# Gates, branches and output projection of a decoder block formed by tokens, residual and second norm by token halves

## The chip, the cores and the metric

One core of a Trainium2 chip runs the kernel. The metric is device time in microseconds of one execution, as a median of several runs. The engines that matter here are TensorE (PE in the profile, with PEld for its weight loads), VectorE (DVE), ScalarE (ACT) and the queue of SyncE (SPq), which issues most transfers. All of them run their own instruction lists in order and wait for each other by semaphores. Results of TensorE go to PSUM banks of 128 x 512 float32.

## The reference

One decoder block on 256 tokens of width 2048, in float32:

```python
xn = rmsnorm(x, norm_mix_pre)
proj = einsum('bsd,dc->bsc', xn, w_in)
mq, mk, mv, mo, mi, mf, aq, ak, av, g_m, g_a = split_cols(proj)
h_m = (normed mLSTM of conv(mq, mk), mv, mi, mf) * sigmoid(mo)
h_a = block attention of rope(aq), rope(ak), av
merged = sigmoid(g_m) * (h_m @ w_branch_m) + sigmoid(g_a) * (h_a @ w_branch_a)
x = x + rmsnorm(merged @ w_out, norm_mix_post)
u = square(relu(rmsnorm(x, norm_ffn_pre) @ w_up))
x = x + rmsnorm(u @ w_down, norm_ffn_post)
```

The widths: mq, mk, mv, mo, aq, ak, av are 1024 each, the gates g_m and g_a, merged and the output 2048 each, u 8192.

## The kernel before

Every float32 product is made of three products of a higher and a lower part (hi x hi, lo x hi, hi x lo) in a format that TensorE takes fast. So each weight unit of 1 MB (128 x 2048) is loaded by SyncE's queue into one of three raw buffers, ACT casts each half to whi (L169), and DVE subtracts to get wlo (L170). There are four buffers for each, so the weights run one to two units ahead of TensorE.

A product is made in one of two forms. In the feature form (`mm_feat`), the weights are the stationary side and 256 tokens the moving side, hi and lo of the activations side by side: one 512-column matmul (L188) and one of 256 (L189) for each 128 input features. The result has output features on partitions and tokens along the row. `mm_feat_one` does the same with three 256-column matmuls (L215 to L217), into one half of a bank. In the token form (`mm_tok`, L200 to L205), 128 tokens are the stationary side and 512 output columns of the weights the moving side: three 512-column matmuls for each 128 input features and token half. Its result has tokens on partitions; rms scales per token are then per-partition scalars, and whoever wants the features on partitions has to transpose.

The steps run one after another: the products of av, of q and k with attention head by head, of mv, mo, mq, mk with the mLSTM, then gates (`gate_post`), branches (`branch_step`) and the output projection (`feat_step(wo[c], mgmov, ...)`). Before, mo, both gates, both branches and the output projection are in the feature form, one unit of 128 output features at a time. Merged activations come out as needed by the output projection, which has them as its moving side. The sums of squares of its output over features are formed on TensorE with a column of ones. After the last unit (`last_mix`), the scale 1/rms is formed (sums, square root on ACT, a Newton step on DVE), broadcast by a product with the identity (L291), while `keep_warm` puts products of ones (L144) on TensorE. `residual` then goes over 16 feature blocks and makes the normed input hw of the MLP, and the first four up-units run interleaved behind it. `x1_squares` sums the squares for the second norm on TensorE, and `open_mlp` transposes the residual to tokens (L745), 32 transposes. The MLP's down products use seven products instead of eight per group (`group`), a token form with factors xs; the change leaves it as it is, except for the buffers that it takes.

The order on each engine is set by a scheduler, which follows the program's dependences and expected times; what is marked with `keep_in_program_order` keeps its place among the marked instructions. ACT needs another function table for Sin, for Sqrt and for Exp (ACT_TABLE_LOAD); a tiny square root named warm (L678) brings Sqrt's table in ahead of the first use.

## Time and profile before

| | |
|---|---|
| median of 3 runs | 1439.17 us (1438.96 to 1439.21) |
| profiled execution, own time | 1440.65 us |
| its span in the profile | 1438.9 us |
| mean granted TensorE clock | 0.998 of full speed |
| TensorE busy | 1415.9 us (98%) |
| DVE busy | 1148.0 us (80%) |
| ACT busy | 816.2 us (57%) |
| moved by DMA | 281.65 MB, 196 GB/s |

The table says how full each engine is. A full engine is not an engine at its peak, since ends of matmuls are modelled; so the distance from one matmul's start to the next is what a pace is read from. The chain of work that ended last says which engine the end of the span depended on, and the idle time ahead of a group of instructions says what it waited for.

### The profile page before, as it was taken

The page shows a single profiled execution, that of the slowest core. Times are in us where ns is not written, and L with a number is a line of the kernel's source. Part 1 is how long each engine was busy: PE and PEld are TensorE (multiplying, and loading weights), DVE is VectorE, ACT ScalarE, POOL GpSimd, SP SyncE. Part 2 cuts the span into 40 slices and gives each one's busy share as a digit, 9 for nine tenths or more (in the row PEclk, how much of TensorE's full clock was granted, in tenths as well). Part 3 has the DMA queues.
Part 4 walks back from the last instruction along what each step waited for, and adds up shares of the span by engine and source line. Part 5 has one row for each costly group of instructions (what it writes and reads, how often), then busy time and mean ns, then how long its engine had stood idle before and what let it go on. Part 6 is the DMA issues. An engine that isn't in the chain of part 4 may idle for free.

```text
span 1438.9 us, 21795 instructions
## 1 busy us (share of the span) xinstructions
PE 1415.9 (98%) x8578; PEld 1253.8 (87%) x8578; DVE 1148.0 (80%) x1607; ACT 816.2 (57%) x1200; POOL 14.5 (1%) x26
## 2 busy tenths in 40 slices
PE   9999999999999999999999999999999999999997
PEld 7888888888888888888899989989889898888975
DVE  7777766776676666665687899898999989999985
ACT  7655465565555444455656565564655655565561
POOL 0000000000000000000000000000000000000000
PEclk9999999999999999999999999999999999999999
DMA  8644444444445545555627665657646667665651
GB/s 258 218 176 176 174 165 161 175 174 176 176 176 182 200 177 195 184 183 197 236 76 247 236 216 179 253 197 263 226 151 242 219 217 239 212 205 193 237 202 59
DMA packets 44167, 281.65 MB, mean 196 GB/s; under 512 B 5024, under 2 KB 7328, under 8 KB 11424
## 3 DMA queue, kind: packets, MB, share of 16 engines
q1 hardware_dynamic: 41904, 265.57, 49.6%
q0 software_dynamic: 2016, 14.68, 5.5%
q8 instruction: 67, 1.10, 0.3%
q14 instruction: 36, 0.29, 0.1%
q10 hardware_dynamic: 144, 0.01, 0.0%
HBM read 278.14 MB, written 2.10 MB: 195 GB/s over the span
## 4 chain that ended last, share of the span: by engine, by line
PE 85%; DVE 11%; issue 2%; ACT 1%; DMA 1%; SPq 0%; DVEq 0%; ACTq 0%
PE acc L188 27%; PE acc L189 14%; PE acc L217 7%; PE acc L215 7%; PE acc L216 7%; DVE wlo L170 6%; PE acc L232 5%; PE acc L226 5%; PE acc L230 5%; PE acc L200 2%; PE acc L205 2%; PE acc L204 2%; DVE xs L774 1%; DVE rawl L862 1%; ACT whi L169 1%
## 5 line engine op out<-in xcount | busy, mean ns | idle before, releaser
L169 ACT CAST whi<-raw 128x1024 fp32r<-128x1024 f32 (+2 forms) x420 | 425.3, 1017 | 420.1 <-PE acc L188 179.1
L170 DVE TENSOR_TENSOR wlo<-raw,whi 128x1024 fp32r<-128x1024 f32 (+2 forms) x420 | 495.0, 1181 | 208.4 <-ACT whi L169 198.0
L188 PE MATMUL acc<-xw,whi 128*128 128x512 f32 x1152 | 408.9, 395 | 0.0
L189 PE MATMUL acc<-xw,wlo 128*128 128x256 f32 x1152 | 328.6, 285 | 0.0
L217 PE MATMUL acc<-hw,wlo 128*128 128x256 f32 x992 | 279.9, 283 | 4.9 <-DVE wlo L170 4.9
L216 PE MATMUL acc<-hw,whi 128*128 128x256 f32 x992 | 279.2, 282 | 0.0
L215 PE MATMUL acc<-hw,whi 128*128 128x256 f32 x992 | 277.7, 282 | 0.0
L188 PEld LDWEIGHTS acc<-xw,whi 128*128 128x128 f32 x1152 | 216.4, 188 | 50.3 <-issue 2.1
L169 ACT CAST whi<-rawl 128x1024 fp32r<-128x1024 f32 x168 | 173.5, 1048 | 116.8 <-PE acc L216 52.2
L189 PEld LDWEIGHTS acc<-xw,wlo 128*128 128x128 f32 x1152 | 216.7, 188 | 0.9
L170 DVE TENSOR_TENSOR wlo<-rawl,whi 128x1024 fp32r<-128x1024 f32 x168 | 201.8, 1218 | 8.4 <-ACT whi L169 6.5
L217 PEld LDWEIGHTS acc<-hw,wlo 128*128 128x128 f32 x992 | 186.9, 188 | 9.9 <-DVE wlo L170 7.3
L215 PEld LDWEIGHTS acc<-hw,whi 128*128 128x128 f32 x992 | 186.0, 188 | 4.6 <-DVE t L757 0.2
L216 PEld LDWEIGHTS acc<-hw,whi 128*128 128x128 f32 x992 | 186.8, 188 | 2.0
L226 PE MATMUL acc<-whi,xs 128*128 128x512 f32 x440 | 174.8, 397 | 2.9 <-ACT whi L169 2.9
L232 PE MATMUL acc<-wlo,xs 128*128 128x512 f32 x440 | 172.4, 397 | 1.8 <-DVE wlo L170 1.8
L230 PE MATMUL acc<-whi,xs 128*128 128x512 f32 x440 | 173.7, 395 | 0.0
L232 PEld LDWEIGHTS acc<-wlo,xs 128*128 128x128 f32 x440 | 82.6, 188 | 21.0 <-DVE wlo L170 4.5
L226 PEld LDWEIGHTS acc<-whi,xs 128*128 128x128 f32 x440 | 82.7, 188 | 20.7 <-ACT whi L169 6.0
L230 PEld LDWEIGHTS acc<-whi,xs 128*128 128x128 f32 x440 | 82.7, 188 | 18.1
L188 PE MATMUL acc<-mg,whi 128*128 128x512 f32 x240 | 84.2, 393 | 0.0
L189 PE MATMUL acc<-mg,wlo 128*128 128x256 f32 x240 | 67.7, 283 | 0.0
(258 smaller groups left out, 1622.1 us busy)
## 6 DMA issues: line engine op xcount, KB each, us to landing
raw<-in_wi_dram SPq DMA_DIRECT2D x96, 1024.0 KB, 4.8
raw<-in_wu_dram SPq DMA_DIRECT2D x64, 1024.0 KB, 6.2
rawl<-in_wd_dram SPq DMA_DIRECT2D x42, 1024.0 KB, 7.8
raw<-in_wd_dram SPq DMA_DIRECT2D x22, 1024.0 KB, 4.9
raw<-in_wo_dram SPq DMA_DIRECT2D x16, 1024.0 KB, 4.8
rawl<-in_wd_dram POOLq DMA_DIRECT2D x14, 1024.0 KB, 10.7
raw<-in_wa_dram SPq DMA_DIRECT2D x8, 520.0 KB, 4.6
raw<-in_wa_dram SPq DMA_DIRECT2D x16, 256.0 KB, 4.7
```

Of the source, the lines that this page charges most:

```text
L169: S.copy(out=hi[:, s], in_=r)
L170: V.tensor_tensor(out=lo[:, s], in0=r, in1=hi[:, s].bitcast(F32), op=ALU.subtract)
L188: PE.matmul(out=accs[i][:, 0:2 * T], lhsT=hi, rhs=m, start=k == 0, stop=False)
L189: PE.matmul(out=accs[i][:, 0:T], lhsT=lo, rhs=m[:, 0, :], start=False, stop=k == nk - 1)
L200: first = PE.matmul(out=acc, lhsT=m[:, 0, ts], rhs=hi, start=start and k == 0, stop=False)
L204: PE.matmul(out=acc, lhsT=m[:, 1, ts], rhs=hi, start=False, stop=False)
L215: PE.matmul(out=acc, lhsT=hi, rhs=m[:, 0, :], start=k == 0, stop=False)
L216: PE.matmul(out=acc, lhsT=hi, rhs=m[:, 1, :], start=False, stop=False)
L217: PE.matmul(out=acc, lhsT=lo, rhs=m[:, 0, :], start=False, stop=k == KT - 1)
L226: first = PE.matmul(out=acc, lhsT=f[:, k, 0], rhs=hi, start=start and k == 0, stop=False, skip_group_check=more)
L230: PE.matmul(out=acc, lhsT=f[:, k, 1], rhs=hi, start=False, stop=False, skip_group_check=more)
L232: PE.matmul(out=acc, lhsT=f[:, k, 0], rhs=lo, start=False, stop=stop and k == 3, skip_group_check=more)
```

## The change

Mo, both gates, both branches and the output projection go to the token form, with weights laid out for it by the host. The gates' and branches' results use the three small PSUM banks (`sm_tile`) in turn, and the tanh of a gate reads its bank directly, with half the token's 1/rms (rhalf) as scale. Merged activations are transposed in blocks of 512 features (`merged`), after branch m of block 2 for three blocks together and at the end for the fourth. A copy of x by tokens is loaded beside xT (`x1_load`), and the post-norm weights are broadcast to all partitions. Sums of squares come from ACT's accumulator (`square`). The last two weight units of the output projection's last block run half 0 first (24 matmuls), then `residual(0)`, then half 1, then `residual(1)`; each residual adds in four blocks of 512, transposes them, and forms hw's hi on ACT and lo on DVE from PSUM. `first_up` takes two units instead of four. The function `seven_steps` is there but SGATES is empty, so it is never called. Cut to its core:

```diff
+def mo_evac(b, h, acc):
+    S.activation(out=so[b][:, h], in_=acc, func=AF.Tanh, scale=rhalf[:, h:h + 1])
+def gate_steps(c, n):
+    for u in range(4):
+        tok_step(wg["ma".index(n), c, u], ("g", n, c), xmov, u,
+                 lambda h, acc: tanh(gate(n, c)[:, h], acc, h), bank=sm_tile)
+def branch_steps(c, n):
+    def evac(h, acc):
+        g = gt[n, c][:, h]
+        V.scalar_tensor_tensor(out=g, in0=g, scalar=1.0, in1=acc, op0=ALU.add, op1=ALU.mult)
+        if n == "m":
+            V.tensor_tensor(out=g, in0=g, in1=gt["a", c][:, h], op=ALU.add)
+    for u in range(2):
+        tok_step(wbr["am".index(n), c, u], ("b", n, c), lambda k: src[:, k], u, evac, last=1,
+                 bank=sm_tile)
+def merged(c):
+    for q in range(2):
+        ps = sm_tile()
+        for j in range(2):
+            for h in range(2):
+                b = 2 * j + h
+                PE.transpose(out=ps[:, b * P:(b + 1) * P],
+                             in_=src[:, h, (2 * q + j) * P:(2 * q + j + 1) * P],
+                             identity=ident)
+        hi, lo = (m[:, 2 * q:2 * q + 2, i] for i in range(2))
+        p = ps.rearrange("p (k t) -> p k t", t=T)
+        S.activation(out=hi, in_=p, func=AF.Copy, scale=0.5)
+        V.scalar_tensor_tensor(out=lo, in0=p, scalar=0.5, in1=hi.bitcast(F32), op0=ALU.mult,
+                               op1=ALU.subtract)
+both_gates(3, (branch_steps, 1, "m"), (branch_steps, 2, "a"), (branch_steps, 2, "m"))
+then(lambda: [merged(c) for c in range(3)])
+branch_steps(3, "a")
+branch_steps(3, "m")
+then(merged, 3)
...
+def mix_evac(e, h, acc):
+    square(acc, late["ssm"][:, h, e:e + 1])
+    V.tensor_tensor(out=late["mix"][e][:, h], in0=acc,
+                    in1=late["wm"][:, e * 512:(e + 1) * 512], op=ALU.mult)
+    if e == 0 and h == 0:
+        S.activation(out=tiny.tile([P, 2], F32, name="warm", tag="warm"), in_=rhalf,
-            S.activation(out=tiny.tile([P, 2], F32, name="warm", tag="warm"), in_=sq[:, 0:2],
                          func=AF.Sqrt)
+def residual(h):
+    pin = tc.keep_in_program_order
+    mix_evac(3, h, late["acc"][h])
+    rms(v, late["ssm"][:, h])
+    rsqrt_act(r, v, 1)
+    for e in range(5):
+        if e < 4:
+            pin(V.scalar_tensor_tensor(out=x1[:, h, es], in0=late["mix"][e][:, h], scalar=r,
+                                       in1=x1[:, h, es], op0=ALU.mult, op1=ALU.add))
+            ps = late["ps", e] = sm_tile()
+            for j in range(4):
+                PE.transpose(out=ps[:, j * P:(j + 1) * P], in_=x1[:, h, k * P:(k + 1) * P],
+                             identity=ident)
+        for j in range(4) if e else ():
+            S.activation(out=hw[:, k, 0, hs], in_=p, func=AF.Copy, scale=g)
+            pin(V.scalar_tensor_tensor(out=hw[:, k, 1, hs], in0=p, scalar=g,
+                                       in1=hw[:, k, 0, hs].bitcast(F32), op0=ALU.mult,
+                                       op1=ALU.subtract))
+    for e in range(4):
+        square(x1[:, h, e * 512:(e + 1) * 512], late["ss2"][:, h, e:e + 1])
+def last_mix():
+    def mm(units):
+        for h in range(2):
+            for i in range(2):
+                mm_tok(late["acc"], units[i], mgmov, 8 + 4 * i, False, i == 1, halves=(h,))
+            if h == 0:
+                residual(0)
+    def post():
+        keep_warm(8)
+        residual(1)
+        open_mlp()
-feat_step([wu[c] for c in range(4)], hmov, first_up, after_k=x1_squares, tail=4,
-          product=mm_feat_one)
+feat_step([wu[0], wu[1]], hmov, first_up, tail=4, product=mm_feat_one)
```

What this makes of the engines' lists is seen at three places. The first is ACT's list in the rope stage, from the scaling of the first av results (av, from the banks acc) on; sinr and cosr are the rope tables, whi the casts of the next weights. Before:

```order
L561 ACTIVATE av_116<-acc_191,rcol_89 128x512 [waits DVE_49]
L561 ACTIVATE av_116<-acc_192,rcol_89 128x512
L561 ACTIVATE av_116<-acc_378,rcol_89 128x260
L561 ACTIVATE av_116<-acc_379,rcol_89 128x260 [waits PE_49]
L293 COPY rbc_90<-sm_529 128x256 [waits PE_49]
L335 ACTIVATE cosr_91<-t256_610 128x256 [waits DVE_49]
L169 CAST whi_642<-raw_640 128x520 [waits DMAHW1_49,PE_49,Activation_49]
L169 CAST whi_646<-raw_640 128x520 [waits PE_49,Activation_49]
```

and now:

```order
L574 ACTIVATE av_116<-acc_194,rcol_87 128x512 [waits DVE_49]
L574 ACTIVATE av_116<-acc_195,rcol_87 128x512
L574 ACTIVATE av_117<-acc_381,rcol_87 128x260
L574 ACTIVATE av_117<-acc_382,rcol_87 128x260 [waits PE_49]
L866 ACT_TABLE_LOAD
L866 ACTIVATE warm_5526<-rhalf_88 128x2 [waits DVE_49]
L299 COPY rbc_90<-sm_532 128x256 [waits PE_49]
L344 ACT_TABLE_LOAD
L344 ACTIVATE cosr_91<-t256_615 128x256 [waits DVE_49]
L175 CAST whi_647<-raw_645 128x520 [waits DMAHW2_49,PE_49,Activation_49]
L175 CAST whi_651<-raw_645 128x520 [waits PE_49,Activation_49]
```

The tiny square root now stands here with a table load, and a second load brings Sin's table back ahead of cosr and the casts.

The second place is TensorE's list at the end of branch m of block 2 (sm_5108 and sm_5107 are its banks, m_3743, m_3884 and m_4307 the merged blocks of tokens, sm_5226 the bank of the next branch product):

```order
L210 MATMUL sm_5108<-whi_5103,hm_95 128x512
L211 MATMUL sm_5108<-wlo_5104,hm_95 128x512
L797 MATMUL sm_5172<-ident_79,m_3743 128x128 x4
L797 MATMUL sm_5179<-ident_79,m_3743 128x128 [waits DVE_49]
L797 MATMUL sm_5187<-ident_79,m_3884 128x128 [waits DVE_49]
L797 MATMUL sm_5194<-ident_79,m_3884 128x128 [waits DVE_49]
L797 MATMUL sm_5202<-ident_79,m_4307 128x128 [waits DVE_49]
L797 MATMUL sm_5209<-ident_79,m_4307 128x128 [waits DVE_49]
L206 MATMUL sm_5226<-whi_5135,ha_94 128x512 [waits DVE_49]
L210 MATMUL sm_5226<-whi_5135,ha_94 128x512
```

Before, where the branches end and the output projection begins (mg0 to mg7 are the merged activations), there was nothing in between:

```order
L189 MATMUL acc_6201<-hm_95,wlo_6139 128x256
L188 MATMUL acc_6201<-hm_95,whi_6138 128x512
L189 MATMUL acc_6201<-hm_95,wlo_6139 128x256
L188 MATMUL acc_6257<-mg0_4182,whi_6192 128x512 [waits DVE_49,Activation_49,Pool_49]
L189 MATMUL acc_6257<-mg0_4182,wlo_6193 128x256 [waits DVE_49]
L188 MATMUL acc_6257<-mg0_4182,whi_6192 128x512
```

Twenty-four transposes into six banks now stand between two streams (the rows with x3 that follow each waiting one are left out), and the next branch waits for a bank. On DVE the same place reads as follows (mg_5171, mg_5186 and mg_5201 are the low halves of the merged blocks):

```order
L780 SCALAR_TENSOR_TENSOR m_4307<-m_4307,sm_5107 128x512 [waits PE_49]
L780 SCALAR_TENSOR_TENSOR m_4307<-m_4307,sm_5108 128x512 [waits PE_49]
L782 TENSOR_TENSOR m_4307<-m_4307,a_4448 128x512 [waits DVE_49] x2
L176 TENSOR_TENSOR wlo_5223<-raw_5216,whi_5222 128x1024 [waits Activation_49]
L803 SCALAR_TENSOR_TENSOR mg_5171<-sm_5172,mg_5171 128x2x256 [waits Activation_49]
L803 SCALAR_TENSOR_TENSOR mg_5171<-sm_5179,mg_5171 128x2x256 [waits Activation_49]
L803 SCALAR_TENSOR_TENSOR mg_5186<-sm_5187,mg_5186 128x2x256 [waits Activation_49]
L803 SCALAR_TENSOR_TENSOR mg_5186<-sm_5194,mg_5186 128x2x256 [waits Activation_49]
```

All that the banks wait for stands behind the gating of m_4307 and a weight's low half.

The third place is TensorE's list from the last output projection matmuls to the first up-matmul (hw is the MLP's input). Before:

```order
L217 MATMUL acc_7027<-mg7_6187,wlo_6969 128x256
L144 MATMUL sm_7079<-ones_83 128x128 x3
L280 MATMUL sm_7083<-ones_83,sq_115 128x2 [waits DVE_49]
L280 MATMUL sm_7083<-ones_83,t256_7076 128x2 [waits Activation_49]
L144 MATMUL sm_7097<-ones_83 128x128 x6
L291 MATMUL sm_7104<-ident_82,rcol_89 128x128 [waits DVE_49,PE_49]
L291 MATMUL sm_7104<-ident_82,rcol_89 128x128
L144 MATMUL sm_7108<-ones_83 128x128 [waits PE_49]
L144 MATMUL sm_7108<-ones_83 128x128 x11
L215 MATMUL acc_7260<-hw_7141,whi_7123 128x256 [waits Activation_49]
```

and now (acc_5831 is the bank of token half 0, acc_5832 that of half 1, x1_5415 the residual by tokens):

```order
L211 MATMUL acc_5831<-wlo_5874,mg_5362 128x512
L891 MATMUL sm_5957<-ident_79,x1_5415 128x128 [waits DMAHW6_49,DVE_49]
L891 MATMUL sm_5957<-ident_79,x1_5415 128x128 x3
L891 MATMUL sm_5963<-ident_79,x1_5415 128x128 [waits DVE_49,PE_49]
L891 MATMUL sm_5963<-ident_79,x1_5415 128x128 x3
L891 MATMUL sm_5977<-ident_79,x1_5415 128x128 [waits DVE_49,PE_49]
L891 MATMUL sm_5977<-ident_79,x1_5415 128x128 x3
L891 MATMUL sm_5991<-ident_79,x1_5415 128x128 [waits DVE_49]
L891 MATMUL sm_5991<-ident_79,x1_5415 128x128 x3
L206 MATMUL acc_5832<-whi_5859,mg_5201 128x512
L210 MATMUL acc_5832<-whi_5859,mg_5201 128x512
```

The transposes of half 0's residual stand ahead of the first matmul of half 1. ACT's list behind half 0's last matmul is now:

```order
L852 ACTIVATE q512_5942,ssm_5520<-acc_5831 128x512 [waits PE_49,Activation_49]
L275 ACT_TABLE_LOAD
L275 ACTIVATE rs_y_5949<-f_v_5945 128x1 [waits DVE_49]
L852 ACTIVATE q512_6012,ss2_5521<-x1_5415 128x512 [waits DVE_49,Activation_49]
L852 ACTIVATE q512_6014,ss2_5521<-x1_5415 128x512 [waits DVE_49,Activation_49]
L896 ACTIVATE hw_5916<-sm_5957,sm_in_84 128x128 [waits PE_49]
L896 ACTIVATE hw_5916<-sm_5963,sm_in_84 128x128 [waits PE_49]
L896 ACTIVATE hw_5916<-sm_5957,sm_in_84 128x128 [waits DVE_49] x3
```

The table load for the square root is in this chain, and each further high half of a bank waits for DVE.

## Rows read from the trace of the kernel before

**Rows 1.** The page: busy time and share of each engine, and the chain's shares.

```profile
PE 1415.9 (98%) x8578; PEld 1253.8 (87%) x8578; DVE 1148.0 (80%) x1607; ACT 816.2 (57%) x1200; POOL 14.5 (1%) x26
...
PE 85%; DVE 11%; issue 2%; ACT 1%; DMA 1%; SPq 0%; DVEq 0%; ACTq 0%
```

**Rows 2.** The page's costly groups: busy us, mean ns, idle ahead and releaser.

```profile
L217 PE MATMUL acc<-hw,wlo 128*128 128x256 f32 x992 | 279.9, 283 | 4.9 <-DVE wlo L170 4.9
```

**Rows 3.** Timeline of PE, feature form: start us, us, engine line op.

```profile
639.66 0.40 PE L188 MATMUL acc<-mg,whi 128*128 128x512 f32 x1
...
649.85 0.39 PE L188 MATMUL acc<-mg,whi 128*128 128x512 f32 x1
```

**Rows 4.** Timeline of PE, token form of the MLP.

```profile
834.75 0.39 PE L232 MATMUL acc<-wlo,xs 128*128 128x512 f32 x1
...
837.31 0.39 PE L230 MATMUL acc<-whi,xs 128*128 128x512 f32 x1
```

**Rows 5.** Timeline of ACT in the rope stage.

```profile
42.57 1.28 ACT L335 ACT_TABLE_LOAD   x1
43.98 0.42 ACT L335 ACTIVATE sinr<-t 128x256 f32<-128x256 f32 x1
...
47.60 2.23 ACT L169 CAST whi<-raw 128x520 fp32r<-128x520 f32 x4
```

**Rows 6.** Timeline of DVE and PE behind these casts.

```profile
48.57 2.53 DVE L170 TENSOR_TENSOR wlo<-raw,whi 128x520 fp32r<-128x520 f32 x4
...
49.35 0.48 PE L205 MATMUL acc<-wlo,xw 128*128 128x260 f32 x2
```

**Rows 7.** Timeline of PE from the output projection to the up-matmuls.

```profile
715.70 0.28 PE L216 MATMUL acc<-mg,whi 128*128 128x256 f32 x1
715.82 0.28 PE L217 MATMUL acc<-mg,wlo 128*128 128x256 f32 x1
...
722.77 0.48 PE L215 MATMUL acc<-hw,whi 128*128 128x256 f32 x2
```

**Rows 8.** Groups of PE by line, 715.9 to 770.

```profile
L217 PE MATMUL acc<-hw,wlo 128*128 128x256 f32 x81 | 22.3, 283 | 0.0
```

**Rows 9.** Timeline of PE where the residual is transposed.

```profile
754.57 1.47 PE L745 MATMUL sm<-ident,x 128*128 128x128 f32 x12
```

**Rows 10.** Timeline of all engines in the tail.

```profile
1429.02 0.40 PE L232 MATMUL acc<-wlo,xs 128*128 128x512 f32 x1
1429.46 0.69 DVE L923 TENSOR_TENSOR y<-acc,y 128x512 f32<-128x512 f32 x1 [3.11 <-PE acc L232]
...
1430.24 0.63 ACT L925 ACTIVATE q<-y 128x512 f32<-128x512 f32 x1 [4.88 <-DVE y L923]
...
1431.24 0.20 ACT L269 ACTIVATE rs_y<-f_v 128x1 f32<-128x1 f32 x1 [0.28 <-DVE f_v L974]
...
1432.26 2.08 DVE L979 SCALAR_TENSOR_TENSOR x<-y,f_r,x 128x512 f32<-128x512 f32 x3
```

**Rows 11.** Groups by line and shape, of all engines.

```profile
L170 DVE TENSOR_TENSOR wlo<-raw,whi 128x1024 fp32r<-128x1024 f32 x388 | 473.3, 1222 | 206.0 <-ACT whi L169 195.9 <-PE acc L189 7.8 <-PE acc L232 0.3
...
L169 ACT CAST whi<-raw 128x1024 fp32r<-128x1024 f32 x388 | 405.9, 1050 | 410.2 <-PE acc L188 179.1 <-PE acc L216 118.3 <-issue 67.7
...
L377 ACT ACTIVATE att_p<-att_p,att_z 128x128 f32<-128x128 f32 x8 | 3.2, 399 | 1.0 <-DVE att_z L376 1.0
...
L474 DVE SCALAR_TENSOR_TENSOR ml_e<-sm,rc,mmask 128x128 f32<-128x128 f32 x4 | 1.4, 341 | 0.0
```

**Rows 12.** Timeline of PE at the start of the span.

```profile
1.06 3.79 PE L144 MATMUL sm<-ones 128*128 128x128 f32 x16 [1.06 <-DVE cv_m L446]
...
6.17 0.63 PE L200 MATMUL acc<-whi,xw 128*128 128x512 f32 x1
6.60 0.52 PE L204 MATMUL acc<-whi,xw 128*128 128x512 f32 x1
```

**Rows 13.** Windows: length, busy us (count) of each engine, PEclk, DMA share, GB/s.

```profile
1433.60:1438.90 5.30, 0.00 (x0) 0.00 (x0) 1.40 (x3) 0.00 (x0) 0.00 (x0) 0.50 0.59 198
```

More of the change, by code (lines that the diff above doesn't have):

```diff
@@ L118, in tile_hybrid_block @@
     sm_in = const.tile([P, S_N], F32, name="sm_in")
-    x = px.tile([P, KT, T], F32, name="x")
+    xh = [k8(f"x{i}").rearrange("p (k t) -> p k t", t=T) for i in range(2)]
     rcol = const.tile([P, 2], F32, name="rcol")
+    rhalf = const.tile([P, 2], F32, name="rhalf")
+    mnh = const.tile([P, 8], F32, name="mnh")
     rbc = const.tile([P, T], F32, name="rbc")
@@ L338, in rope_tables @@
                         op0=ALU.mult)
[L341 to L344 removed]
+    av = [g4("av") for _ in range(2)]
+    mv = [g4("mv", (2, 2, MD + 2)) for _ in range(2)]
+    for m in mv:
+        V.memset(m[:, :, :, MD:MD + 2], 1.0)
     def t384(name):
@@ new lines, in mixed @@
+    def mixed(first, *parts):
+        global_steps = steps[:]
+        del steps[:]
+        for f, *args in parts:
+            f(*args)
+        others = steps[:]
+        steps[:] = global_steps
+        n, done = len(others), 0
+        for i, s in enumerate(first):
+            steps.append(s)
+            while done < n and (done + 1) * len(first) <= (i + 1) * n + len(first) // 2:
+                steps.append(others[done])
+                done += 1
+        steps.extend(others[done:])
@@ L718, in tile_hybrid_block, with square @@
-    for c in range(KT - 1):
-        feat_step(wo[c], mgmov, lambda acc, c=c: mix_post(c, acc))
-    def mm_last(units):
-        late["acc"] = acc_tile()
-        mm_feat_one([late["acc"]], [units[0]], mgmov)
-    steps.append(([wo[KT - 1]], mm_last, last_mix))
+        return mg[k // 4][:, k % 4]
+    def square(src, out):
+        q = pool["f"].tile([P, 512], F32, name="q512", tag="v", bufs=1)
+        S.activation(out=q, in_=src, func=AF.Square, accum_out=out)
+    def mix_evac(e, h, acc):
+        if e == 0 and h == 0:
+            late["mix"] = {}
+            for n in ("ssm", "ss2"):
+                late[n] = const.tile([P, 2, 4], F32, name=n)
+        if h == 0:
+            late["mix"][e] = g4("mix")
+        square(acc, late["ssm"][:, h, e:e + 1])
+        V.tensor_tensor(out=late["mix"][e][:, h], in0=acc,
+                        in1=late["wm"][:, e * 512:(e + 1) * 512], op=ALU.mult)
+        if e == 0 and h == 0:
+            S.activation(out=tiny.tile([P, 2], F32, name="warm", tag="warm"), in_=rhalf,
+                         func=AF.Sqrt)
@@ new lines, in x1_load, with mm @@
+    def x1_load():
+        late["wm"] = k8("wm")
+        nc.sync.dma_start(out=late["wm"], in_=wmix.partition_broadcast(P))
+        late["x1"] = pa.tile([P, 2, D], F32, name="x1", tag="ha")
+        for h in range(2):
+            nc.sync.dma_start(out=late["x1"][:, h], in_=xtok[h])
+    def last_mix():
+        def mm(units):
+            late["hw"] = pa.tile([P, KT, 2, T], F32R, name="hw", tag="xw")
+            late["acc"] = tok_acc["o", 3]
+            for h in range(2):
+                for i in range(2):
+                    mm_tok(late["acc"], units[i], mgmov, 8 + 4 * i, False, i == 1, halves=(h,))
+                if h == 0:
+                    residual(0)
[3 more added lines that the diff above has]
+            open_mlp()
+        steps.append(([wo[14], wo[15]], mm, post))
@@ L940, in place @@
                 late["wd"] = pa.tile([P, 2, 2, 2, 1024], F32R, name="wd", tag="xw")
-            return late["wd"][:, v]
+            return [(late["wd"][:, v, h, 0], late["wd"][:, v, h, 1]) for h in range(2)]
         places[len(steps)] = place
```

405 lines of the change are left out of this document (226 added, 179 removed).

## The prediction

> **What bounds the kernel now.** I read the engine table and the shares of the chain first. PE is busy for 1415.9 of 1438.9 us and carries 85% of the chain that ends last [rows 1]; DVE's 11% and ACT lie beside it. Next come the idle times in the table of costly groups: the largest wait of any matmul group is 4.9 us in all, on the low halves of the weights [rows 2], and all PE waits together are about 14 us. So there is hardly a wait to win. Only three things can move the end: how many columns PE streams and at what pace, what stands between two streams and is itself not streaming, and any stall that the new order puts before PE. The rest of the argument is a hunt for those three along the order of the changed kernel. The sum is made against the profiled execution, 1440.65 us, which is 1.5 us above the median of 1439.17; I take 1.5 us off at the end.
>
> **1. Streaming by tokens.** A feature pair (512 and 256 columns) starts every (649.85 - 639.66) / 29 = 0.3514 us [rows 3]. A 512-column matmul of the token form starts every (837.31 - 834.75) / 11 = 0.2327 us [rows 4]. Three of these do the work of two pairs: 0.698 against 0.703 us. Gates, output gates, branches and all of the output projection but its last unit were 1136 of the 1648 pairs and become 568 triples: 568 x 0.0048 = 2.7 us less at this pace, and 1.0 less if the token step costs 0.2334. I take -2.2. The columns are the same, so nothing more is in it.
>
> **2. A table load that moves into the rope stage.** The dummy square root ("warm") took a late square as input; now it takes rhalf, which is ready with rcol, ahead of the rope tables. In the changed order ACT does it there: a table load, the square root, then another load to get Sin back, both ahead of cosr and of four weight casts. A load is 1.28 us [rows 5], a square root 0.2 [rows 10], so 2 x 1.28 + 0.2 = 2.8 us on ACT. Before, the casts ran from 47.60 with no idle time ahead [rows 5]; DVE's low halves followed from 48.57, and a matmul took the first of them at 49.35 [rows 6]: four take 2.53 us, one some 0.7, so the slack is about 0.1 us. This piece of PE's order is the same, so the 2.8 us go through to PE: +2.8. If PE had slack that I don't see, 0. The row of a load shows it follow the cast at once and the Sin 1.41 us after the load's start [rows 5]. The Trainium skill ("ScalarE: Activation LUTs", What ACT_TABLE_LOAD costs) adds a drain of 1.38 us to each switch; by it this term would be 5.5 us. The trace here shows no such drain.
>
> **3. Transposes of the merged branches.** Merged activations are now formed by tokens and must be turned before the output projection. Merged(0) to merged(2) stand in a row on PE after branch m of block 2: 24 transposes into six tiles, in a ring of three small PSUM banks. Transposes start every 0.12 us (1.47 for 12, [rows 9]), so 2.9 us is the least. But a bank comes free only after ACT's high half and DVE's low half, and the next branch matmul needs the bank of the fourth tile. DVE's queue from the last matmul before: 0.4 until its result can be read [rows 10]; then one of the two gatings of m still open (0.7) and two additions (1.4), a weight's low half (1.22, [rows 11]), four low halves of merged tiles (0.7 each, all priced by DVE's 128 x 512 steps, [rows 10]): 0.4 + 0.7 + 1.4 + 1.2 + 2.8 = 6.5 us, against 0.23 for a normal next matmul. That is +6.3, transposes included; ACT's six high halves, each about as long as the tail's Square (0.63, [rows 10]), fit inside. It is 2.9 if DVE's queue were free and 8 if ACT and DVE can't read two banks at once. Merged(3) is followed by matmuls that don't need it: 8 x 0.12 = +0.9.
>
> **4. Residual and second norm.** Before, PE goes from the last output matmul at 715.82 to the first up-matmul at 722.77 [rows 7]. From 715.9 to 770 it did 339 up-matmuls (three groups of 81, one of them in [rows 8], and six of 16) at 0.12 us, the step of the last output matmuls [rows 7], 40.5 us of 54.1: 13.6 us not streaming.
>
> The change says that residual(0) runs beside the matmuls of half 1. PE's order says otherwise: all 16 transposes of residual(0) stand ahead of the 24 matmuls of half 1. PE is in order, so these wait for the whole chain of half 0:
> - From the last matmul of half 0: 0.44 to its result, 2.02 from Square to the residual's first step [rows 10], and about 1.0 for the table load that is now inside this chain (1.28, of which 0.3 lies beside DVE): 3.5 us.
> - Two residual steps (0.7 each) and two Squares (0.8 each, with the read of the sum) on ACT, partly side by side, bring the first high half to 5.9 us.
> - High and low halves of one bank alternate, since each next high half waits for the low half before. 0.40 on ACT and 0.34 on DVE [rows 11] with 0.05 for the two hand-overs are 0.79 us a block, a low price, since the tail's hand-over from DVE to Square takes 0.09 [rows 10]. The last tile's residual step stands behind eight of them: 8 x 0.79 + 2 x 0.7 = 7.7, then four transposes, 0.5. The sum is 14.1, less 0.23: 13.8 us without streaming.
> - Half 1 then takes 24 x 0.233 = 5.6 us, and after it the chain repeats. Queued ahead of it are a cast that needs the last weight buffer of half 1 (1.05) and its low half (1.22, [rows 11]): 0.44 + 1.05 + 1.22 + 0.34 (a low half still open) + 0.7 (times the weights) + 1.4 (the sums and the square root, 2.02 less the Square and 0.2 more for a reduction, [rows 10]) + 0.7 + 0.5 + 0.4 = 6.7 us. With free queues it would be about 4.
> - The up-matmuls then walk k at the pace of the 16 alternations of half 1 (16 x 0.79 + 1.4 = 14 us) while four interleaved units offer 22.9 us of work; by the place of the last waits about 11 us can be done by then. I put 3 us of starving and 1.0 for transposes in between, 0 to 6.
>
> Together 13.8 + 6.7 + 4.0 = 24.5, less 13.6: +10.9, from +3 (free queues, 0.6 a block) to +17.
>
> **5. The clock.** PE does next to nothing for some 13 us in that place. In the tail the record shows the granted clock at 0.50, the 1.2 GHz level, from 1433.60 on, when PE's last matmul had started at 1429.02 [rows 10, 13]; at the start of the span, where PE works from 1.06 us on, 512-column matmuls are still 0.43 us apart at 6.17 to 6.60 [rows 12], 1.2 GHz by their pace. If half 1 starts at 1.2 GHz, each of its matmuls costs 0.2 us more. If it lasts as it did there, some 6 us, 14 of the 24 are slow: +2.7; all 24 are +4.7; none is 0. I take +2.7, since the tail's fall came after a pause shorter than this one. "TensorE: Matmul & The Clock Gate" (Part 1) of the Trainium skill has the low level as the default that activity lifts, which speaks against this change; the tail agrees.
>
> **6. Nothing.** The new transfers (2 MB of x, 1 MB of broadcast weights) are behind the queue's weights by some units and are wanted much later. Gate and branch steps share three banks, but 18 or more matmuls of half 0 (4 us) stand between the use of one and the next; a gating takes 0.7. The last stage, the attention and the MLP keep their instructions. I put 0 here, with 0 to 3 for the range.
>
> **Sum.** 1440.65 - 2.2 + 2.8 + 6.3 + 0.9 + 10.9 + 2.7 = 1462.1; less 1.5: **1461 us**, 1.5% slower.
>
> **The rivals.**
> - Not slower: half 1 really covers residual(0). Then the 13.8 us fall to the 16 transposes (1.9), and the stretch costs 1.9 + 6.7 + 4 = 12.6, -1.0 against before; no clock loss. If the merged tiles also cost only their transposes (2.9) and the table loads are hidden, 1440.65 - 2.2 + 3.8 - 1.0 - 1.5 = 1440; with free queues behind half 1 (4 us and no starving) 1434. It decides if the high and low halves are not waited for by half 1. For it: the program is written so. Against it: PE's order has the transposes ahead, and the last of them need the eighth alternation. I give it 0.12.
> - The residual alone is cheaper: order as I read it, but blocks alternate at 0.6 us, the queues behind half 1 are free and the clock holds: 1440.65 - 2.2 + 2.8 + 6.3 + 0.9 + 3 - 1.5 = 1450. 0.18.
> - More stalls: PE runs at 1.2 GHz through half 1 and into the first up-matmuls (+4.7 and some 3 more), ACT and DVE exclude each other in the merged tiles (8): 1440.65 - 2.2 + 2.8 + 8 + 0.9 + 14 + 7.7 - 1.5 = 1470. 0.2.
> - My forecast, 1455 to 1466: 0.5.
>
> **How the numbers follow.** Below about 1445 lies most of the first rival; above 1473 a tenth of the third and what I missed. The range is 1445 to 1473. A difference under 0.2% (2.9 us) can't be told from no change. Faster takes about half of the first rival, 0.06; same the other half, 0.05; slower 0.89.
>
> **What would show it.** Right: two more table loads near 47 us and a PE gap of 2 to 3 us at the next low half; a hole of 6 us on PE between branch m of block 2 and branch a of block 3, released by DVE's low halves; a hole of 13 to 14 us ahead of half 1, one of 7 us ahead of the first up-matmul, and PEclk below 9 in that slice. Wrong: half 1's matmuls running beside the residual's steps, or more than 3 us of new waits in the gates or in the attention, which I put at nothing.

## The result, and the profile after

The changed kernel takes 1496.41 us (median of four runs, 1494.37 to 1497.34) against 1439.19 us before (1438.96 to 1439.87): ratio 1.0395, 95% interval 1.0377 to 1.0413. It is slower, as forecast, but by 57 us and not by 22; the range ended at 1473. The profiled execution took 1497.34 us with a span of 1495.6 and a mean granted clock of 0.977 (before 0.998).

The page of after, answering [rows 1] and [rows 2]: busy time and share of each engine, the chain's shares, and the costliest matmul group with idle time ahead of it (busy us, mean ns, idle us and what ended it).

```profile
PE 1438.9 (96%) x7964; PEld 1242.4 (83%) x7964; DVE 1098.5 (73%) x1432; ACT 783.6 (52%) x1071; POOL 14.5 (1%) x26
...
PE 89%; DVE 7%; ACT 2%; issue 1%; DMA 0%; DVEq 0%; SPq 0%; ACTq 0%
...
L232 PE MATMUL acc<-whi,xs 128*128 128x512 f32 x440 | 176.1, 401 | 17.6 <-ACT whi L175 17.6
```

PE is busy 23 us longer with the same columns, so much of that is work at a lower clock, and its largest wait by group has moved to the MLP's down products, for casts on ACT. Yet the page alone hides how much is lost where. So I added up, over all matmul rows of each trace, how far the distance from one matmul's start to the next exceeds the usual step of its shape (0.2325 us for 512 columns, 0.1195 for 256, 0.120 for 260); every other matmul counts in full. What comes out is time in which PE did not stream, transposes and slow steps included. With the streaming itself (1361.0 us before, 1357.1 after) and 1.06 us before the first matmul it gives the span:

| us not streaming | before | after | change | predicted |
|---|---|---|---|---|
| 0 to 60 (rope stage at 47) | 8.3 | 12.5 | +4.2 | +2.8 |
| 60 to 400 (attention, mLSTM, first gates) | 31.1 | 42.7 | +11.6 | 0 |
| 400 to 700 (gates, branches, output projection) | -0.3 | 11.2 | +11.5 | +7.2 |
| transition to the MLP (700 to 780) | 13.5 | 24.7 | +11.2 | +13.6 |
| MLP and tail | 24.2 | 46.2 | +22.0 | 0 |
| streaming | 1361.0 | 1357.1 | -3.9 | -2.2 |
| sum of the changes | | | +56.6 | +21.4 |

The two lines that I put at zero hold 33.6 of the 35 us that the forecast missed. The stages are those of one trace of each kernel, and the four runs of after lie 3 us apart.

**What I had seen.** Timeline of PE in after at the residual, where [rows 7] stood before (start us, us, engine line op, and in brackets the idle time ahead and its releaser):

```profile
733.77 0.39 PE L211 MATMUL acc<-wlo,mg 128*128 128x512 f32 x1
738.08 1.97 PE L891 MATMUL sm<-ident,x 128*128 128x128 f32 x8 [3.92 <-DVE x L886]
743.48 1.09 PE L891 MATMUL sm<-ident,x 128*128 128x128 f32 x4 [3.42 <-DVE x L886]
747.11 1.11 PE L891 MATMUL sm<-ident,x 128*128 128x128 f32 x4 [2.55 <-DVE x L886]
747.88 0.78 PE L206 MATMUL acc<-whi,mg 128*128 128x512 f32 x1
...
754.88 0.40 PE L211 MATMUL acc<-wlo,mg 128*128 128x512 f32 x1
...
761.49 0.77 PE L221 MATMUL acc<-hw,wu 128*128 128x256 f32 x2
```

Half 1 begins at 747.88, 14.11 us behind the last matmul of half 0: 13.9 without streaming, where I had 13.8. Its last matmul starts at 754.88, and the first up-matmul at 761.49. The same engine between branch m of block 2 and branch a of block 3:

```profile
619.37 1.60 PE L797 MATMUL sm<-ident,m 128*128 128x128 f32 x12
623.25 1.85 PE L797 MATMUL sm<-ident,m 128*128 128x128 f32 x12 [2.29 <-DVE mg L803]
625.32 0.80 PE L206 MATMUL sm<-whi,ha 128*128 128x512 f32 x1 [0.22 <-DVE mg L803]
```

The hole is 5.95 us long (619.37 to 625.32). ACT in the rope stage, answering [rows 5], where cosr's scaling and the casts followed at once:

```profile
47.35 1.28 ACT L866 ACT_TABLE_LOAD   x1
48.64 0.20 ACT L866 ACTIVATE warm<-rhalf 128x2 f32<-128x2 f32 x1
48.75 0.35 ACT L299 COPY rbc<-sm 128x256 f32<-128x256 f32 x1
49.12 1.28 ACT L344 ACT_TABLE_LOAD   x1
50.42 0.42 ACT L344 ACTIVATE cosr<-t 128x256 f32<-128x256 f32 x1
```

PE then waits for the casts, from the matmul that starts at 48.93 to the next one:

```profile
51.40 0.48 PE L206 MATMUL acc<-whi,xw 128*128 128x260 f32 x1 [2.19 <-ACT whi L175]
```

**What I had not seen.** First, PE around the mLSTM's fourth head (L478 to L505 are its steps, L206 the first gate product):

```profile
359.16 1.19 PE L488 MATMUL sm<-qkm 128*128 128x256 f32 x2 [1.57 <-DVE ml_e L483]
363.68 1.22 PE L488 MATMUL sm<-qkm 128*128 128x256 f32 x2 [3.33 <-DVE qkm L468]
...
368.79 0.99 PE L206 MATMUL sm<-whi,xw 128*128 128x512 f32 x1
```

From 355.97 to 368.79 not one matmul of 512 columns runs. Before, the same head had the gates' feature pairs (L188 and L189, in the large banks) between its steps, one behind the other from 370.07 on and without a wait (L469 and L479 are L478 and L488 there):

```profile
369.23 0.91 PE L469 MATMUL sm<-rows,ident 4*128 4x384 f32 x2
370.07 0.50 PE L188 MATMUL acc<-xw,whi 128*128 128x512 f32 x1
...
376.00 0.59 PE L479 MATMUL sm<-qkm 128*128 128x256 f32 x2
```

Second, DVE, ACT and PE in a group of the MLP (L1038 forms the sum bt of two weight blocks, L175 casts it, L970 makes factors):

```profile
988.17 0.68 DVE L970 TENSOR_TENSOR xs<-s_b,xs 128x512 fp32r<-128x512 f32 x1
...
988.78 2.29 DVE L1038 TENSOR_TENSOR bt<-raw,b 128x2048 f32<-128x2048 f32 x1
...
989.11 0.40 PE L238 MATMUL acc<-wlo,xs 128*128 128x512 f32 x1
...
991.17 1.99 ACT L175 CAST whi<-bt 128x1024 fp32r<-128x1024 f32 x2 [4.14 <-DVE bt L1038]
...
992.27 0.50 PE L232 MATMUL acc<-whi,xs 128*128 128x512 f32 x1 [2.76 <-ACT whi L175]
```

The sum reaches ACT too late, and PE stands still from 989.11 to 992.27. There are six such holes, five of 2.93 and one of 2.66 us beyond a step. Together with the slow steps behind them the six stretches hold some 27.5 us; the loss is less, since five pairs of waits that before has in the MLP (0.6 and 1.1 us each) are gone. Before, the same sum stood well ahead of its use: what it waits for is its data, and no cast waits for it.

```profile
979.18 2.29 DVE L856 TENSOR_TENSOR rawl<-raw,rawl 128x2048 f32<-128x2048 f32 x1 [0.67 <-DMA raw<-in_wd_dram]
```

### The profile page after: what moved, and what is told of

Its sections match the earlier page's. It is cut to its first block, busy times and chain, and to the rows that moved or that the text cites. A ratio compares the mean times of both kernels' runs of the same rounds, so it can differ in the third digit from the quotient of the medians.

```text
span 1495.6 us, 20198 instructions
## 1 busy us (share of the span) xinstructions
PE 1438.9 (96%) x7964; PEld 1242.4 (83%) x7964; DVE 1098.5 (73%) x1432; ACT 783.6 (52%) x1071; POOL 14.5 (1%) x26
## 4 chain that ended last, share of the span: by engine, by line
PE 89%; DVE 7%; ACT 2%; issue 1%; DMA 0%; DVEq 0%; SPq 0%; ACTq 0%
PE acc L223 8%; PE acc L221 8%; PE acc L222 8%; PE acc L194 8%; PE sm L206 6%; PE sm L210 6%; PE sm L211 6%; PE acc L232 6%; PE acc L236 5%; PE acc L238 5%; PE acc L206 5%; PE acc L210 5%; PE acc L211 5%; PE acc L195 4%; DVE wlo L176 2%; ACT whi L175 1%
## 5 line engine op out<-in xcount | busy, mean ns | idle before, releaser
L175 ACT CAST whi<-raw 128x1024 fp32r<-128x1024 f32 (+2 forms) x420 | 425.9, 1017 | 444.3 <-PE sm L210 141.1
L222 PE MATMUL acc<-hw,whi 128*128 128x256 f32 x992 | 283.2, 286 | 0.0
L221 PE MATMUL acc<-hw,whi 128*128 128x256 f32 x992 | 283.1, 286 | 0.0
L221 PEld LDWEIGHTS acc<-hw,whi 128*128 128x128 f32 x992 | 191.2, 193 | 5.2
L223 PEld LDWEIGHTS acc<-hw,wlo 128*128 128x128 f32 x992 | 191.5, 193 | 4.3 <-DVE wlo L176 1.1
L222 PEld LDWEIGHTS acc<-hw,whi 128*128 128x128 f32 x992 | 191.1, 193 | 2.1
L194 PE MATMUL acc<-xw,whi 128*128 128x512 f32 x512 | 183.6, 397 | 0.0
L195 PE MATMUL acc<-xw,wlo 128*128 128x256 f32 x512 | 146.4, 286 | 0.0
L175 ACT CAST whi<-bt 128x1024 fp32r<-128x1024 f32 x84 | 86.0, 1046 | 83.8 <-PE acc L222 28.2
L194 PEld LDWEIGHTS acc<-xw,whi 128*128 128x128 f32 x512 | 96.2, 188 | 23.1 <-issue 2.1
L176 DVE TENSOR_TENSOR wlo<-bt,whi 128x1024 fp32r<-128x1024 f32 x84 | 101.2, 1220 | 13.4 <-ACT whi L175 13.3
L206 PE MATMUL sm<-whi,xw 128*128 128x512 f32 x256 | 102.1, 399 | 0.0
L210 PE MATMUL sm<-whi,xw 128*128 128x512 f32 x256 | 101.6, 397 | 0.0
L211 PE MATMUL sm<-wlo,xw 128*128 128x512 f32 x256 | 100.2, 396 | 0.0
```

The source lines that it names most:

```text
L175: S.copy(out=hi[:, s], in_=r)
L176: V.tensor_tensor(out=lo[:, s], in0=r, in1=hi[:, s].bitcast(F32), op=ALU.subtract)
L194: PE.matmul(out=accs[i][:, 0:2 * T], lhsT=hi, rhs=m, start=k == 0, stop=False)
L206: first = PE.matmul(out=acc, lhsT=m[:, 0, ts], rhs=hi, start=start and k == 0, stop=False)
L210: PE.matmul(out=acc, lhsT=m[:, 1, ts], rhs=hi, start=False, stop=False)
L211: PE.matmul(out=acc, lhsT=m[:, 0, ts], rhs=lo, start=False, stop=stop and k == 3)
```

## The experiments

The theory after the result had four parts: (A) the MLP loses because its four long buffers no longer form one ring (a ring is a set of equal buffers that all allocations under one name share); (B) the mLSTM's last head and the branches lose because gates and branches hold the small banks; (C) the early table loads cost some 4 us; (D) the residual costs what was worked out, through PE's order and the alternation of high and low halves. The rival to A was that the MLP loses by what comes ahead of it (weights late, or another phase of the order), the rival to B that the token form of the gates itself leaves the mLSTM bare.

**Before with its ring of four cut in two.** Only t and b12 get a ring of their own:

```diff
-    def long_raw():
-        return pool["f"].tile([P, 2048], F32, name="rawl", tag="rawl", bufs=4)
+    def long_raw(tag="rawl"):
+        return pool["f"].tile([P, 2048], F32, name=tag, tag=tag, bufs=2)
-            r["12"], r["t"] = long_raw(), long_raw()
+            r["12"], r["t"] = long_raw("rawt"), long_raw("rawt")
```

> The kernel before, with its ring of four long raw buffers cut into two rings of two, one for b12 and t and one for b22 and b21, as the changed kernel has it; nothing else. Theory: the same holes of about 2.9 us ahead of q5 appear in each of the seven blocks, with a half-clock stretch behind each: 3 to 3.5 us a block, 1458 to 1464 us. Rival (the rings are not the cause): 1437 to 1442 us.

Measured: 1469.8 us, ratio 1.0209 (1.0192 to 1.0226), more than expected. Its table of stages is that of before except for the MLP: 54.1 us not streaming for 24.2. The timeline of DVE, ACT and PE shows after's pattern in the kernel of before:

```profile
953.00 2.28 DVE L856 TENSOR_TENSOR rawt<-raw,rawt 128x2048 f32<-128x2048 f32 x1
...
955.39 2.00 ACT L169 CAST whi<-rawt 128x1024 fp32r<-128x1024 f32 x2 [3.31 <-DVE rawt L856]
...
956.49 0.50 PE L226 MATMUL acc<-whi,xs 128*128 128x512 f32 x1 [2.48 <-ACT whi L169]
```

The same four buffers and the same instructions: the cut alone costs 30 us, with nothing changed ahead of the MLP. So the rings are enough to make such a loss. What comes ahead of the MLP in after is tested by the rotation below.

**After with the pairs exchanged.** t shares a ring with b22, b12 with b21:

```diff
-            r["12"], r["t"] = k8("b12"), k8("bt")
+            r["12"], r["t"] = long_raw(), k8("bt")
-            r["22"] = long_raw()
+            r["22"] = k8("b22")
```

> The changed kernel with one thing else: in the MLP's groups the sum t takes its buffer from the same ring of two as b22, and b12 from the same ring as b21, instead of t with b12 and b22 with b21. No memory, no load and no arithmetic changes. Theory (the ring of four raw buffers was cut into two rings of two, so that t of the next group must wait for the last weight split of t in this one, and its 2.28 us sum falls among the factor steps on DVE): the 2.9 us holes on PE ahead of the q5 product, seven of them, and the half-clock stretch behind each go; about 22 us of the MLP's 36 us without streaming fall to 14 to 20: 1475 to 1482 us. Rival (the MLP waits because the factors now share a ring with other tiles, or because the longer stall at the residual shifted DMA against it): 1494 to 1498 us, holes unchanged.

Measured: 1488.76 us, ratio 1.0341 (1.0326 to 1.0357), a miss. The MLP falls from 46.2 to 38.9 only. The big holes go and four waits of 0.6 to 0.9 us come in each of the last five groups. I had expected the partner of t to decide everything; it decides 7 of the 22 us, so the other buffers' places count as well.

**After with the rotation of before written out.** In the addresses of before's four buffers, which no trace shows, t takes the old place of b12, b12 that of b21, b21 that of t, and b22 keeps one. Here three named places rotate like that by hand:

```diff
+        rot = (("k8a", "k8b", "ra"), ("ra", "k8a", "k8b"), ("k8b", "ra", "k8a"))[(2 * j + p) % 3]
-            r["12"], r["t"] = k8("b12"), k8("bt")
+            r["12"], r["t"] = slot("b12", rot[0]), slot("bt", rot[1])
-            r["21"] = long_raw()
+            r["21"] = slot("b21", rot[2])
```

> The changed kernel with the MLP's long raw buffers taken in the rotation that the kernel before has: b12, t and b21 rotate over three places (t takes the place that b12 had in the last group, b12 that of b21), b22 keeps one. The two rings of two become four named places; memory, loads and arithmetic stay. Theory (the cut ring is all that the MLP lost): t's sum moves ahead of the last weight splits of the group before, the 2.9 us holes go, and the MLP's 36.3 us without streaming fall to about 14: 1472 to 1477 us. Rival (half of it is the factors, which now share a ring with the MLP's squares): 1480 to 1486 us.

Measured: 1471.44 us, ratio 1.0218 (1.0203 to 1.0234), 25 us under after and just under what was expected. The MLP is at 22.7 us; another 2.7 us are in the first 60 us of the span (12.5 to 9.8), which this edit does not touch: PE waits there as long as in after, but no slow steps follow (see the last section). By line, what DVE waited for ahead of the sum (L1043 here), us and times:

```profile
  DMA raw<-in_wd_dram: 3.6, 6
```

What comes ahead of the MLP is as in after, so A's rival falls. The sum again waits for nothing but its data, as before, and unlike after, where the list of who waited for the sum (L1038) has

```profile
  ACT whi L175: 23.6, 6
```

That a new t has to wait for the last split of the old one, and so falls behind the factors on DVE, is read from the order of the rows; that the rings are the cause is shown both ways.

**After with gates and branches in the large banks.**

```diff
-                     lambda h, acc: tanh(gate(n, c)[:, h], acc, h), bank=sm_tile)
+                     lambda h, acc: tanh(gate(n, c)[:, h], acc, h))
-            tok_step(wbr["am".index(n), c, u], ("b", n, c), lambda k: src[:, k], u, evac, last=1,
-                     bank=sm_tile)
+            tok_step(wbr["am".index(n), c, u], ("b", n, c), lambda k: src[:, k], u, evac, last=1)
```

> The changed kernel with the gates and branches accumulated in the five large banks instead of the three small ones; nothing else. Theory (products that hold small banks for 48 matmuls keep PE from running them beside the fourth head of the mLSTM, and the transposes of the merged blocks from running beside the next branch): the 13 us of waits around 356 to 369 us fall to 2 to 3, the waits at 588 and 595 (2.6) go, and of the 7.6 us at the merged blocks 3 to 5 go: 1477 to 1483 us. Rival (there is too little other work left at that place, whatever the bank): the mLSTM part stays, 1489 to 1495 us.

Measured: 1479.06 us, ratio 1.0273 (1.0257 to 1.0288), 17 us under after and as expected. Stage 60 to 400 falls from 42.7 to 31.9, 400 to 700 from 11.2 to 3.7. PE at the same head of the mLSTM now:

```profile
361.97 0.91 PE L478 MATMUL sm<-rows,ident 4*128 4x384 f32 x2
362.81 0.50 PE L211 MATMUL acc<-wlo,xw 128*128 128x512 f32 x1
...
367.55 0.59 PE L488 MATMUL sm<-qkm 128*128 128x256 f32 x2
367.79 0.58 PE L210 MATMUL acc<-whi,xw 128*128 128x512 f32 x1
```

Between the head's two products stand 20 gate products (362.81 to 367.55), and there is no wait. The token form is the same, so B holds and its rival falls.

**After with the dummy square root late**, on the first sum of squares of the output projection:

```diff
-            S.activation(out=tiny.tile([P, 2], F32, name="warm", tag="warm"), in_=rhalf,
-                         func=AF.Sqrt)
+            S.activation(out=tiny.tile([P, 2], F32, name="warm", tag="warm")[:, 0:1],
+                         in_=late["ssm"][:, 0, 0:1], func=AF.Sqrt)
```

> The changed kernel with the tiny square root fed by a sum of the output projection, which is formed late, instead of rhalf; nothing else. Theory: the two table loads near 47 us and the one at the first residual go, one comes in the output projection beside matmuls: 4.0 us less at 40 to 60 us and up to 1 us less at the residual, 1491 to 1493 us. Rival (PE's hole at 49 us has another cause, such as the order of the rope tables on DVE): 1495 to 1498 us.

Measured: 1491.97 us, ratio 1.0363 (1.0347 to 1.0378); the first 60 us fall from 12.5 to 8.6. C holds at -3.9. The residual gains nothing from it (24.7 to 26.1).

**After with half 1's matmuls ahead of residual(0), and after with the halves of a bank in turns of four.**

```diff
-                if h == 0:
-                    residual(0)
+            residual(0)
```

> The changed kernel with half 1's 24 matmuls of the output projection written ahead of the first residual, so that no transpose stands between the two halves; nothing else. Theory (in-order PE puts half 1 behind half 0's chain): the 14.1 us hole ahead of half 1 goes, half 1 covers 5.6 us of the chain and runs at full clock, but ACT and DVE still alternate through 32 blocks, so the hole behind half 1 grows: 5 to 8 us less, 1488 to 1491 us. Rival (ACT's and DVE's alternation alone sets the end, PE's order nothing): 1494 to 1497 us.

```diff
                 S.activation(out=hw[:, k, 0, hs], in_=p, func=AF.Copy, scale=g)
+            for j in range(4) if e else ():
+                k, p = 4 * e - 4 + j, late["ps", e - 1][:, j * P:(j + 1) * P]
+                g = sm_in[:, S_FFN + k:S_FFN + k + 1]
                 pin(V.scalar_tensor_tensor(out=hw[:, k, 1, hs], in0=p, scalar=g,
```

> The changed kernel with the four high halves of a transposed tile written ahead of its four low halves, so that ACT and DVE change over once a tile and not once a block; nothing else. Theory (a bank that both read is handed to and fro, 0.79 us a block): the hole ahead of half 1 falls from 14.1 to about 10 us, and the starving of the first up-matmuls by 2 to 3: 6 to 8 us less, 1488 to 1491 us. Rival (the chain is set by the four additions, the squares and the transposes): 1494 to 1497 us.

Measured: 1493.19 us (ratio 1.0368, 1.0352 to 1.0384) and 1490.61 us (1.0358, 1.0341 to 1.0376). In the traces both take 4 us out of the transition (24.7 to 20.7 and 20.8). The median of the first missed its range by 2 us; its runs lie from 1490.08 to 1495.41. So each of the two things that D names, the order and the alternation, is worth 4 us, and neither alone brings the stage back to 13.5. The two together, and nothing else, were not run.

**All of it together.** Rotation, large banks and late square root, and the residual written anew: both halves' blocks in turn behind all matmuls, four highs and then four lows of a bank:

```diff
+            residual([(0, 0), (0, 1)])
             keep_warm(8)
-            residual(1)
+            residual([(1, 0), (1, 1), (0, 2), (1, 2), (0, 3), (1, 3)])
```

> The changed kernel with all of it mended: the rotation of the MLP's buffers (22 us), gates and branches in the large banks (17.4 us), the late square root (4.4 us), and a residual that comes behind both halves of the output projection and goes through the blocks of both token halves in turn, four high and then four low halves a tile. Theory (the causes add up): 1496.4 - 22 - 17.4 - 4.4 = 1452.6 with the old residual; the new one leaves about 5 us of waiting and 4 us of transposes where the changed kernel has 25, so 1436 to 1440 us, at or just under the kernel before. Rival (the causes overlap, or the rotation or the large banks make new waits together): 1443 to 1455 us.

Measured: 1439.98 us (ten runs), ratio 1.0002 (0.9992 to 1.0011): the same as before. By stage 8.3, 32.0, 3.7, 13.0 and 22.9 us. Undoing the four causes takes back the whole loss by the stages (MLP 23.3, mLSTM 10.7 and branches 7.5, rope stage 4.2, transition 11.7), and nothing is won beyond it: the 3.9 us of streaming go to the transposes of the merged tiles (+4.0) and to the mLSTM (+0.9). The transition could still give: DVE between the last matmul of half 0 and its residual (L180 splits weights here, L280 to L264 are the steps of 1/rms):

```profile
713.93 1.23 DVE L180 TENSOR_TENSOR wlo<-raw,whi 128x1024 fp32r<-128x1024 f32 x1 [0.53 <-ACT whi L179]
715.07 0.16 DVE L280 RECIPROCAL rs_y<-rs_y 128x1 f32<-128x1 f32 x1
715.39 1.23 DVE L180 TENSOR_TENSOR wlo<-raw,whi 128x1024 fp32r<-128x1024 f32 x1 [0.16 <-ACT whi L179]
716.53 0.15 DVE L262 SCALAR_TENSOR_TENSOR rs_a<-rs_y 128x1 f32<-128x1 f32 x1
716.78 1.23 DVE L180 TENSOR_TENSOR wlo<-raw,whi 128x1024 fp32r<-128x1024 f32 x1
...
718.18 1.22 DVE L180 TENSOR_TENSOR wlo<-raw,whi 128x1024 fp32r<-128x1024 f32 x1
719.32 0.15 DVE L264 SCALAR_TENSOR_TENSOR f_r<-rs_a,rs_y 128x1 f32<-128x1 f32 x1
```

Four splits of 1.22 us stand between steps of 0.15 us, each of which only has to wait for the one before.

**The chain ahead of the splits.** The same kernel with the steps of 1/rms pinned in program order together with the splits, and, second, with half 1's chain ahead of the highs and lows as well:

```diff
-            rms(v, late["ssm"][:, h])
-            rsqrt_act(r, v, 1)
+            pin(V.reduce_sum(out=v, in_=late["ssm"][:, h], axis=AX.X))
...
+            pin(S.activation(out=y, in_=v, func=AF.Sqrt))
+            pin(V.reciprocal(out=y, in_=y))
```

> The kernel with all of it mended, and its residual's chain (sums, root, Newton steps, first additions) pinned on DVE and ACT ahead of the weight splits of the third and fourth up-unit, which in the mended kernel's trace stand between the Newton steps: four splits of 1.2 us in a chain that takes 2.5 us alone. Nothing else is changed. Theory (these splits hold the chain, 720.4 instead of about 715 us): the wait behind half 1 falls from 3.3 us to none, PE starts the up-matmuls some 5 us earlier and at full clock, 1433 to 1436 us. Rival (the second chain, half 1's, sets the start of the up-matmuls, or the late splits starve the third unit): 1437 to 1441 us.

```diff
-            if last:
-                out(*last)
-            last = h, e
+            wait.append((h, e))
+            if (h, e) == (1, 0):
+                out(*wait.pop(0))
```

> The pinned kernel with half 1's chain written ahead of the first high and low halves of half 0's tiles: in the pinned kernel's trace four low halves that wait for ACT stand ahead of half 1's product with the post-norm weights (720.24, when its bank was ready at 717.3). Nothing else. Theory: half 1's first addition comes 2 to 3 us earlier than 722.2 and the first up-matmul with it (724.6): 1434.5 to 1437 us. Rival (the up-matmuls are then starved by the high and low halves that come later, so that nothing is won): 1438 to 1440 us.

Measured: 1438.37 us (ratio 0.9988, 0.9979 to 0.9997) and 1439.29 us (0.9998, 0.9989 to 1.0007). Both miss what was hoped for. In the first, the transposes of half 0 now follow the last matmul without a wait (0.16-us steps from 713.78 on, first transposes at 717.19), and PE waits a little later:

```profile
717.19 1.04 PE L912 MATMUL sm<-ident,x 128*128 128x128 f32 x8
...
723.08 1.09 PE L912 MATMUL sm<-ident,x 128*128 128x128 f32 x4 [3.06 <-issue]
724.62 0.80 PE L226 MATMUL acc<-hw,wu 128*128 128x256 f32 x2 [0.46 <-ACT hw L922]
```

On DVE of the same kernel half 1's scaling stands behind four lows that wait for ACT:

```profile
719.20 1.12 DVE L924 SCALAR_TENSOR_TENSOR hw<-sm,sm_in,hw 128x128 fp32r<-128x128 f32 x4 [1.90 <-ACT hw L922]
720.24 0.68 DVE L888 TENSOR_TENSOR mix<-acc,wm 128x512 f32<-128x512 f32 x1
```

The second starts half 1's chain earlier (its scaling at 718.20), but on ACT the square root of the chain still stands behind four highs (720.68) and DVE's Newton steps come among lows, so that the first addition is at 722.55, where the first had 722.22. PE has nothing from 720 to 723.4 and its first up-matmul at 725.85. So the edit did not move the step that it was made for, and whether an earlier chain would help is open. That 1438.37 is really below before is at the edge of what this measurement tells, and no version here beats before by 0.2%.

## Why the prediction was right and wrong

**Step 6 failed.** "The last stage, the attention and the MLP keep their instructions. I put 0 here": the instructions stay, but not what they wait for. 36.2 of the 56.6 us come from it:
- *MLP, +22.0.* My account of the kernel says that the change leaves the MLP as it is "except for the buffers that it takes", and no step prices that exception. A ring of four became two rings of two with the same memory. The cut alone costs before 30 us, and the rotation alone gives after 23.5 of its 46.2 back.
- *mLSTM, +11.6.* I had asked whether gate and branch steps wait for each other's banks, but not who else uses the three small banks: the mLSTM's last head, which the gates' matmuls should cover. In large banks 10.8 of it vanish.
- *Banks among branches, +2.6.* "18 or more matmuls of half 0 (4 us) stand between the use of one and the next" was true for the gates, and wrong at two branches, where the gating on DVE comes late: PE steps from 588.38 to 589.57 and from 595.04 to 596.90. That lies inside the 0 to 3 that I left.

With 0 to 3 for this step the range could not hold the result. One of the signs of being wrong was the right one, "more than 3 us of new waits in the gates or in the attention, which I put at nothing": they came between the two, at the mLSTM's last head. In short: an item put at nothing because its instructions are unchanged had no bound from rows.

**The others, in order.** *1, streaming*, -2.2: -3.9 by the usual steps, an error of the pace in the third digit. (At 0.2334 the working gives 1.5 us less, not 1.0.) *2, table loads*, +2.8: the wait is 2.35 us (48.93 to 51.40, less a step of 0.12), and the rest of the 4.0 that the stage loses here is slow steps of 0.22 behind it. By the added drain that the Trainium skill states ("ScalarE: Activation LUTs", What ACT_TABLE_LOAD costs) the term would have been 5.5 by the estimate in the prediction; the second load begins at 49.12 and cosr's scaling at 50.42, 1.30 us later, so the trace shows no drain. *3, merged tiles*, +6.3 and +0.9: the hole is 5.95, and with the slow steps behind it 7.5; the fourth block 0.9. *4, residual*, +10.9: 13.9 ahead of half 1 for 13.8; 6.4 behind it (754.88 to 761.49, less 0.23) for 6.7; but the 4.0 for starved up-matmuls and transposes behind that came to 1.2, mostly transposes. *5, clock*, +2.7: half 1 is slow at first, as said. Its 23 steps take 7.00 us, 1.65 more than usual, and the first up-matmuls are slow too, which adds 1.6. 4 and 5 together are +11.2 for +13.6.

Added up, the steps 1 to 5 gave +21.4, and without what belongs to step 6 the trace has +20.4. So the forecast stands for all that the diff writes out, helped by errors that cancel: the holes are a little shorter, the up-matmuls hardly starve and the streaming a little better than worked out, while the clock costs something behind two more holes (the rope stage and the merged tiles), where I had charged it at one only. That the sum of these steps comes within 1 us is in part luck.

**The rivals.** "Not slower: half 1 really covers residual(0)" is excluded by the rows at 738.08 to 747.88. "The residual alone is cheaper" falls too: the blocks alternate at 0.79 and not 0.6 us, and the clock does not hold. "More stalls" is nearest in its time (1470), and right in that slow steps last into the up-matmuls, but not by its reasons: without step 6's losses after would have been at about 1460 (1496.4 less 36.2), next to the forecast.

## What to carry to other kernels

When a change takes buffers or banks from a pool, list every user of that pool before and after, also in stages whose code is untouched, and ask of each which release its next allocation waits for; "same instructions" is no reason for a zero. Two rings of two are not a ring of four: in one ring, a buffer that is needed early may take any of the four places that has come free, in a ring of two it has to wait for its own pair. And a stall can be followed by slow steps; then it costs more than its length.

## What the runs showed of the hardware

The granted clock behind a hole is seen in after's windows (length; busy us and count of PE, PEld, DVE, ACT and POOL; PEclk; DMA share; GB/s). Around the waits at 588.38 and 595.04, 1.19 and 1.86 us from start to start, it stays up:

```profile
588.00:592.00 4.00, 3.22 (x14) 2.29 (x13) 1.38 (x2) 0.96 (x1) 0.00 (x0) 1.00 0.37 156
595.00:600.00 5.00, 3.54 (x16) 2.55 (x14) 3.49 (x4) 2.31 (x3) 0.00 (x0) 1.00 0.75 249
```

Behind a hole of the MLP (989.11 to 992.27) PE first goes on at the full pace, and only then falls to 0.50, the 1.2 GHz level, while it streams:

```profile
992.20:993.60 1.40, 1.33 (x9) 1.24 (x10) 1.40 (x3) 0.96 (x2) 0.23 (x1) 1.00 0.64 181
993.60:997.00 3.40, 3.40 (x18) 3.40 (x18) 3.40 (x5) 1.18 (x3) 0.00 (x0) 0.50 0.99 272
997.00:1000.00 3.00, 3.00 (x26) 3.00 (x26) 3.00 (x4) 1.04 (x2) 0.00 (x0) 0.99 1.03 251
```

The steps of 256 columns are 0.12 us at 993.4, 0.21 from 993.69 to 996.89, and 0.12 after it: 15 steps, 1.4 us, nearly half of the hole's own length once more. I had known the low clock from the tail and the start of the span alone and had not expected that it comes behind the work's return.

Not every hole is followed by it. PE's wait in the rope stage is 2.47 or 2.48 us from start to start in all six kernels that keep the early square root: after, and after with the pairs exchanged, the rotation, the large banks, the other order and the turns of four. The granted clock falls behind it in four of the six traces and stays up with the rotation and with the turns. The first line is after's, the second that of the rotation:

```profile
51.30:54.00 2.70, 2.60 (x11) 2.43 (x12) 2.65 (x5) 1.64 (x4) 0.00 (x0) 0.55 0.09 18
49.80:53.00 3.20, 2.90 (x22) 2.70 (x22) 2.79 (x5) 2.59 (x4) 0.00 (x0) 1.00 0.20 23
```

Of the six holes of the MLP (2.90 to 3.16 us from start to start) all are followed by it in after, five with the large banks, five with the turns and four with the other order. The four runs of after fit this: the fastest, 1494.37 us, shows a granted clock of 0.982, the slowest, 1497.34 us, one of 0.977.

High and low halves of one bank, on ACT and DVE in turn, start 0.79 us apart (ACT's highs at 741.13 and 741.92), which was the estimate; four and four in turn take 4 us less in the whole stage.
